# Totals of the adaLN vectors over the partitions: VectorE transposes and row sums with one 32-column matmul, in place of eight one-column matmuls

## The chip, the cores and the metric

One core of one Trainium2 chip runs the whole program. The metric is the device time of one execution in microseconds (us); the kernel before took 1523.76 us, the median of 3 runs between 1518.08 and 1527.92.

## The reference, cut to what matters

The program is one inference step of a two-layer hybrid backbone. It has 128 context tokens and 256 latent tokens of width 2048. Each layer multiplies normalised tokens by a large input projection (2048 x 7184), runs four branches (a linear recurrence, neighbourhood attention, grouped attention, a matrix memory) and goes through an output projection (2048 x 2048). What the change touches is the adaLN modulation:

```python
mod = jax.nn.silu(cond) @ lp['ada_w'] + lp['ada_b']
shift, scale, gate = jnp.split(mod, 3, axis=-1)
xm = rmsnorm(x, lp['norm_w']) * (1.0 + scale) + shift
...
x = x + gate * y
```

There are two conditioning vectors (context and latent), so per layer this is a product of 2 x 2048 with 2048 x 6144, all in float32. The input projection needs scale and shift of a channel before it can read it; the output step needs the gate.

## The kernel before, in words

**Large matmuls.** Both projections run on TensorE in three float32 passes (high x high, low x high, high x low), issued by `block` (line 1321) and, for the last 256 output columns, by `mm` (line 1362). The weights arrive in `raw`; ScalarE writes their high part `wh` (line 190 is the helper `act`), GpSimd their low part `wl` (line 1218). Tokens are modulated channel block by channel block in `modulate`: VectorE writes `xmt` and the low part `xl` (line 194 is the helper `stt`), ScalarE the high part `xh`.

**The adaLN vectors.** The 6144 outputs of a layer are cut into 12 sets of 512 columns: sets 0 to 7 hold shift and scale for 256 channels each, sets 8 to 11 the gate. Set 0 of layer 0 is made on TensorE (`ada_pe`). The other 23 sets are made on VectorE. For each of the 16 blocks of 128 input rows the weights `araw` (128 x 512) are multiplied by the conditioning value of each partition and added to an accumulator in PSUM, `sbp`: `ada_dve` puts two such pieces, one for each conditioning vector c, into a list called `backlog`. The last piece of a set writes to SBUF (`adasb`, 128 x 1024) instead. What is left is the total over the 128 partitions. `ada_final` (line 300) makes it with eight matmuls: each takes 128 columns of `adasb` as the stationary operand and one column of ones as the moving one, so that 128 totals come out as a column in PSUM. Line 305 adds the bias into `mod`, and one more instruction makes `Amul` for the scales.

**What sets the order.** A list called `plan` interleaves the visits of the projection with the adaLN pieces: 2.5 blocks per visit in layer 0, 2.0 in layer 1 (`RATE`), so that the vectors for the next channel group are due three visits ahead (`LAG`). After each block of matmuls `tick` takes an eighth of the backlog, at least one entry, and starts each final whose time has come (`FLAG` later than its last piece). Where a visit needs a channel that is not modulated yet, `need` and `ada_wait` empty the backlog and run the finals at that place. Layer 0 reads its channels in groups of 2, 2, 2, 2, 4 and 4 blocks (`KG`), and needs sets 1 to 7 during its first pass over the weights. Layer 1 has two groups of 8 blocks; its sets 0 to 3 and the gates of layer 0 run beside the later part of layer 0. Each engine then works through its own queue in order. While layer 0 makes its first sums the final's PSUM bank is also one that the projection uses (`final_bank`), so that the next block waits until VectorE has read it.

**Start.** The constants `cst` (identity and ones, 128 x 256) are loaded from ScalarE's queue (line 1463) while SyncE's queue loads conditioning, adaLN weights and tokens.

Of the kernel before, what the change touches and what calls it, by code (L numbers as in the profile page):

```python
# [9 lines left out]
F32 = mybir.dt.float32  # L10
F32R = mybir.dt.float32r
AF = mybir.ActivationFunctionType
OP = mybir.AluOpType
AX = mybir.AxisListType
# [4 lines left out]
T = TP + TS  # L19
DEPTH = 2  # L20
# [10 lines left out]

CC = {}
_n = 0
for _name, _w in (("ident", 128), ("ones", 128), ("u", 128), ("l", 128), ("mf", 128), ("mb", 128),
                  ("cos", 256), ("sin", 256), ("nam", 64)):
    CC[_name] = (_n, _n + _w)
    _n += _w
# [8 lines left out]
PP_W = _n  # L46
# [3 lines left out]
def shape_consts():  # L50
    a = np.zeros((128, CC_W), np.float32)
    p = np.arange(128)

    def put(name, v):
        a[:, CC[name][0]:CC[name][1]] = v

    put("ident", np.eye(128))
    put("ones", 1.0)
    put("u", p[:, None] <= p[None, :])
    put("l", p[:, None] >= p[None, :])  # L60
    put("mf", np.where(p[:, None] > p[None, :], BIG, 0.0))
    put("mb", np.where(p[:, None] < p[None, :], BIG, 0.0))
    qc, kc = p % 64, np.arange(64)
    st = np.clip(qc - 8, 0, 48)[:, None]
    put("nam", np.where((kc[None] >= st) & (kc[None] < st + 16), 0.0, NEG))
    inv = np.float32(10000.0) ** (-np.arange(32, dtype=np.float32) / np.float32(32))
    t = np.arange(256)
    ang = [(q.astype(np.float32)[:, None] * inv).astype(np.float32) for q in (t // 64, t % 64)]
    cos = np.concatenate([np.cos(ang[0]), np.cos(ang[0]), np.cos(ang[1]), np.cos(ang[1])], 1)
    sin = np.concatenate([-np.sin(ang[0]), np.sin(ang[0]), -np.sin(ang[1]), np.sin(ang[1])], 1)  # L70
    put("cos", cos.reshape(2, 128, 128).transpose(1, 0, 2).reshape(128, 256))
    put("sin", sin.reshape(2, 128, 128).transpose(1, 0, 2).reshape(128, 256))
    return a
# [3 lines left out]
def tile_hybrid_step(ctx: ExitStack, tc: tile.TileContext, I, O):  # L77
    nc = tc.nc
    ps_space = bass.MemoryType.PSUM
    consts = ctx.enter_context(tc.tile_pool(name="consts", bufs=1))  # L80
# [3 lines left out]
    wrk = ctx.enter_context(tc.tile_pool(name="wrk", bufs=1))  # L84
# [6 lines left out]
    FLAG = 4.0  # L91
# [12 lines left out]
    clock = dict(now=0.0, due=0.0)  # L104
    deferred = []
    backlog = []
# [36 lines left out]
    def sm(i, n, name):  # L143
        return wrk.tile([128, n], F32, name=name, tag=f"m{i}", bufs=2)

    pers_all = consts.tile([128, T + 256 + PP_W + DEPTH * 128 + 256], F32, name="pers")
    used = [0]

    def pers(n):
        used[0] += n  # L150
        return pers_all[:, used[0] - n:used[0]]

    cst = pers(256)
    prm = pers(PP_W)
    nc.sync.dma_start(prm[:, :PP_1], I["prm"][:, :PP_1])

# [3 lines left out]
    def C(n):  # L160
        return cst[:, CC[n][0]:CC[n][1]]

    def P(n, l=None, parts=2):
        a, b = PP[n]
        if l is None:
            return prm[:, a:b]
        s = (b - a) // parts
        return prm[:, a + l * s:a + (l + 1) * s]

    ident = C("ident")  # L170
    ones = C("ones")
# [16 lines left out]
    def act(out, in_, f, bias=0.0, scale=1.0, accum=None):  # L188
        if accum is None:
            return nc.scalar.activation(out, in_, f, bias=bias, scale=scale)  # L190
        return nc.scalar.activation(out, in_, f, bias=bias, scale=scale, accum_out=accum)  # L191

    def stt(out, a, s, b, op0, op1):
        return nc.vector.scalar_tensor_tensor(out, a, s, b, op0=op0, op1=op1)  # L194
# [41 lines left out]
    ada_acc = dict(done=0)  # L236
    last_ev = {}

    def order(later, earlier):
        tc.add_manual_dep(later, earlier.name,  # L240
                          mybir.DependencyInfo(mybir.DependencyClass.NoSync, mybir.DependencyReason.DATA),
                          reason="issue order")
# [22 lines left out]
    sbp = pada.tile([128, 1024], F32, name="sbp")  # L265

    def ada_pe(it):
# [8 lines left out]
        if it["stop"]:  # L276
# [7 lines left out]
                ada_final_mod(0, j0, 2)  # L284
            ada_acc["done"] += 1

    finals = []
    rot = [True]

    def final_bank():  # L290
        if not rot[0]:
            return scr("adaf")
        turn[0] += 1
        return (accb[3], sbank[1])[turn[0] % 2]

    def ada_final(l, s, part):
        pt = final_bank()
        for q in range(4):
            for c in range(2):
                nc.tensor.matmul(pt[:, 2 * q + c:2 * q + c + 1], part[:, c * 512 + q * 128:c * 512 + q * 128 + 128],  # L300
                                 ones[:, 0:1], start=True, stop=True)
        pv = pt[:, 0:8].rearrange("p (q c) -> p q c", c=2)
        for j0, q0, n in (((2 * s, 0, 2), (16 + 2 * s, 2, 2)) if s < 8 else ((4 * s, 0, 4),)):
            b = P("ada_b", l)[:, j0:j0 + n]
            nc.vector.tensor_tensor(mod[:, l, j0:j0 + n, :], pv[:, q0:q0 + n, :],  # L305
                                    b[:, :, None].to_broadcast([128, n, 2]), op=OP.add)
            if 16 <= j0 < 32:
                nb = P("norm", l)[:, j0 - 16:j0 - 16 + n]
                stt(Amul[:, l, j0 - 16:j0 - 16 + n, :], mod[:, l, j0:j0 + n, :], 1.0,
                    nb[:, :, None].to_broadcast([128, n, 2]), OP.add, OP.mult)  # L310
        ada_acc["done"] += 1
        ada_acc[l, s] = True
# [5 lines left out]
    def ada_dve(it):  # L318
        raw = it["raw"]

        def piece(c):
            it["left"] -= 1
            l, s, k = it["l"], it["s"], it["k"]
            acc = sbp[:, c * 512:(c + 1) * 512]
            sc = scond[:, k, c:c + 1]
            if it["start"]:
                d = nc.vector.tensor_scalar(acc, raw, sc, None, op0=OP.mult)
            elif not it["stop"]:
                d = stt(acc, raw, sc, acc, OP.mult, OP.add)
            else:  # L330
                if c == 0:
                    ada_acc["part"] = wrk.tile([128, 1024], F32, name="adasb", tag="adasb", bufs=1)
                part = ada_acc["part"]
                d = stt(part[:, c * 512:(c + 1) * 512], raw, sc, acc, OP.mult, OP.add)
                if c == 1:
                    finals.append((clock["now"] + FLAG, lambda: ada_final(l, s, part)))
            if "v" in last_ev:
                order(d.ins, last_ev["v"])

        it["left"] = 2  # L340
        for c in range(2):
            backlog.append(lambda c=c: piece(c))

    def ada_wait(ok):
        while not ok():
            if backlog:
                drain_backlog(1)
            elif finals:
                run_finals(True)
            else:  # L350
                run_deferred(True)
# [1109 lines left out]
            pos[key] += 1  # L1461

    nc.scalar.dma_start(cst, I["cst"])
    act(warm, scond[:, 0, 0:1], AF.Sqrt, bias=epsc, scale=0.0)
    pos["a"] = n_first
    xq = [range(k, k + 4) for k in range(0, KC, 4)]
    for tok in START:
        if tok == "x":
            for k in xq[0]:
                nc.sync.dma_start(xr[k], I["xT"][:, k, :])  # L1470
            for k in xq.pop(0):
                square_in(k, xr[k], nc.vector)
        elif tok == "w":
            upto("w", wl, w_dma, pos["w"] + 1)
        elif tok == "r":
            rstd_bc()
        elif tok == "P":
            it = first.pop(0)
            a_dma(it)
            ada_pe(it)  # L1480
        elif tok == "D":
            it = a_items[pos["a"]]
            upto("a", a_items, a_dma, pos["a"] + 1)
            ada_dve(it)
            it["early"] = True
# [4 lines left out]
    for it in plan:  # L1490
# [3 lines left out]
        if ty == "a":  # L1494
            upto("a", a_items, a_dma, it["i"] + NADA - 1)
            (ada_pe if it["mode"] == "pe" else ada_dve)(it)
        elif ty == "mod":
            l = it["l"]
# [19 lines left out]
        else:  # L1518
# [6 lines left out]
            if open_banks and PRE[it["l"]] and not it["first"]:  # L1525
                open_banks = False
                for t in [accb[nb] for nb in PREB] + [sbank[0]]:
                    nc.tensor.matmul(t, xh[0][:, 0:128], xh[0][:, 0:1].to_broadcast([128, 512]),
                                     start=True, stop=True)
# [22 lines left out]
def lay_out(inp):  # L1552
# [36 lines left out]
    put("m0", f["state_mlstm_m"][0].reshape(1, -1))  # L1589
    a["prm"] = p  # L1590
    k = shape_consts()
    a["cst"], a["mlk"], rope, nam = np.split(k, (CC["u"][0], CC["cos"][0], CC["nam"][0]), 1)
    a["gqk"] = np.stack([np.concatenate([rope, np.broadcast_to(f["gqa_qnorm"][l], (128, 128)),
# [49 lines left out]
```

## Time and profile before

| | before |
|---|---|
| median of 3 runs | 1523.76 us |
| profiled execution, its own time | 1518.68 us |
| its span on the core | 1516.9 us |
| TensorE matmul (PE) busy | 1448.2 us, 95% |
| VectorE (DVE) busy | 1003.0 us, 66% |
| GpSimd (POOL) busy | 930.0 us, 61% |
| ScalarE (ACT) busy | 793.5 us, 52% |
| mean granted TensorE clock | 0.976 |

Busy shares are of the span. A profile gives each instruction's start and duration, and for an engine that stood idle the instruction or transfer that ended the wait. Matmuls overlap each other, so the time that one takes of TensorE is read from start to start, not from its duration. A float32 matmul shows as two passes, each with its own weight load.

### The profile page before, as it was taken

To read this page: it belongs to the slowest core of one execution; us is meant where nothing else is said; L and a number is where in the kernel's file an instruction comes from. 1 tells how busy PE (TensorE), PEld (TensorE's weight loads), DVE (VectorE), ACT (ScalarE), POOL (GpSimd) and SP (SyncE) were. 2 spreads that over 40 slices of the span, in tenths; PEclk is the share of its full clock that TensorE was granted. 3 is DMA by queue.
4 is the path that set the end of the run, shared out by engine and by line. 5 is a ranking of instruction groups with operands and counts; after the bars stand their busy time and mean duration, and the time that the engine had idled before them with its cause. 6 is when DMAs were issued, how large, how long until landed. Compare 5 with 4: busy or idle time off the path is not lost. (4 is left out here: it accounts for less than half of the span.)

```text
span 1516.9 us, 24338 instructions
## 1 busy us (share of the span) xinstructions
PE 1448.2 (95%) x8321; PEld 1364.1 (90%) x8321; DVE 1003.0 (66%) x1858; ACT 793.5 (52%) x1613; POOL 930.0 (61%) x1270
## 2 busy tenths in 40 slices
PE   6999989999997899999999999999999989899997
PEld 1989979999986798999998999999999869899997
DVE  4988988887759777655558995644844864643423
ACT  4689945664456773632334343233444876364432
POOL 1656655656657658556647665775656775845762
PEclk7999989999999999999999999999999999999999
DMA  8877867866646474476747886654545445435543
GB/s 278 269 246 231 253 203 234 258 189 196 173 124 181 122 224 135 150 231 218 251 140 255 254 254 181 188 165 120 155 138 154 130 134 164 138 103 184 180 126 95
DMA packets 167165, 281.64 MB, mean 186 GB/s; under 512 B 17216, under 2 KB 48960, under 8 KB 166912
## 3 DMA queue, kind: packets, MB, share of 16 engines
q1 hardware_dynamic: 159520, 272.40, 58.6%
q10 hardware_dynamic: 7296, 7.42, 1.5%
q8 instruction: 65, 1.06, 0.3%
q14 instruction: 60, 0.49, 0.1%
q0 software_dynamic: 224, 0.27, 0.1%
HBM read 271.11 MB, written 8.93 MB: 185 GB/s over the span
## 5 line engine op out<-in xcount | busy, mean ns | idle before, releaser
L1218 POOL TENSOR_TENSOR wl<-raw,wh 128x256 fp32r<-128x256 f32 (+1 forms) x1152 | 857.9, 777 | 496.7 <-ACT wh L190 450.8
L1321 PE MATMUL acc<-xh,wh 128*128 128x384 f32 x1634 | 564.4, 346 | 13.2 <-ACT xh L190 6.7
L1321 PE MATMUL acc<-xl,wh 128*128 128x384 f32 x1634 | 556.4, 340 | 1.2 <-DVE xl L194 1.2
L1321 PE MATMUL acc<-xh,wl 128*128 128x384 f32 x1634 | 553.2, 339 | 2.4 <-POOL wl L1218 2.4
L190 ACT ACTIVATE wh<-raw 128x1024 fp32r<-128x1024 f32 (+2 forms) x304 | 307.1, 1014 | 408.4 <-PE acc L1321 331.0
L194 DVE SCALAR_TENSOR_TENSOR sbp<-araw,pers,sbp 128x512 f32<-128x512 f32 x644 | 484.0, 752 | 21.9 <-DMA araw<-in_ada_n 8.8
L1321 PEld LDWEIGHTS acc<-xh,wh 128*128 128x128 f32 x1634 | 308.9, 189 | 18.5 <-ACT xh L190 7.9
L1321 PEld LDWEIGHTS acc<-xh,wl 128*128 128x128 f32 x1634 | 308.6, 189 | 3.8 <-POOL wl L1218 3.5
L1321 PEld LDWEIGHTS acc<-xl,wh 128*128 128x128 f32 x1634 | 309.2, 189 | 2.8 <-DVE xl L194 1.5
L1321 PE MATMUL acc<-wh,xl 128*128 128x512 f32 (+2 forms) x454 | 165.2, 364 | 3.4 <-DVE xl L194 3.1
L1321 PE MATMUL acc<-wh,xh 128*128 128x512 f32 (+2 forms) x454 | 164.1, 362 | 0.0
L1321 PE MATMUL acc<-wl,xh 128*128 128x512 f32 (+2 forms) x454 | 162.9, 359 | 0.0
L1321 PEld LDWEIGHTS acc<-wh,xl 128*128 128x128 f32 x454 | 87.3, 192 | 17.7 <-DVE xl L194 4.8
L1321 PEld LDWEIGHTS acc<-wl,xh 128*128 128x128 f32 x454 | 87.7, 193 | 11.3
L1321 PEld LDWEIGHTS acc<-wh,xh 128*128 128x128 f32 x454 | 87.7, 193 | 10.6
L194 DVE SCALAR_TENSOR_TENSOR cat<-acc,pers,xold 128x128 f32<-128x128 f32 (+1 forms) x56 | 20.6, 409 | 111.9 <-PE acc L1321 111.8
L190 ACT ACTIVATE xh<-xmt,pers 128x128 fp32r<-128x128 f32 x72 | 29.0, 430 | 41.0 <-DVE xmt L194 40.9
L190 ACT ACTIVATE cat<-acc 128x384 f32<-128x384 f32 (+1 forms) x78 | 38.3, 496 | 6.8 <-PE acc L1321 6.0
L300 PEld LDWEIGHTS s<-pers,adasb 128*128 128x128 f32 x304 | 37.3, 193 | 2.3 <-ACT arena L191 1.7
L305 DVE TENSOR_TENSOR pers<-s,pers 128x4 f32<-128x4 f32 (+1 forms) x30 | 4.0, 158 | 50.7 <-PE s L300 47.7
L300 PE MATMUL s<-pers,adasb 128*128 128x1 f32 x304 | 35.7, 246 | 1.4 <-DVE adasb L194 1.3
L194 DVE SCALAR_TENSOR_TENSOR xl<-xmt,pers,xh 128x128 fp32r<-128x128 f32 x72 | 35.3, 511 | 1.7 <-ACT xh L190 1.6
(334 smaller groups left out, 1823.3 us busy)
## 6 DMA issues: line engine op xcount, KB each, us to landing
raw<-in_w_in SPq DMA_DIRECT2D x208, 512.0 KB, 3.9
araw<-in_ada_n SPq DMA_DIRECT2D x368, 256.0 KB, 4.3
raw<-in_w_out SPq DMA_DIRECT2D x64, 512.0 KB, 3.7
raw<-in_w_in SPq DMA_DIRECT2D x32, 256.0 KB, 3.0
araw<-in_ada_n SPq DMA_DIRECT2D x8, 512.0 KB, 5.6
xr<-in_xT SPq DMA_DIRECT2D x16, 192.0 KB, 5.1
nac<-in_nac SPq DMA_DIRECT2D x8, 288.0 KB, 4.1
xold<-in_xT SPq DMA_DIRECT2D x3, 768.0 KB, 6.3
```

The source lines that it names most:

```text
L190: return nc.scalar.activation(out, in_, f, bias=bias, scale=scale)
L194: return nc.vector.scalar_tensor_tensor(out, a, s, b, op0=op0, op1=op1)
L300: nc.tensor.matmul(pt[:, 2 * q + c:2 * q + c + 1], part[:, c * 512 + q * 128:c * 512 + q * 128 + 128], ones[:, 0:1], start=True, stop=True)
L305: nc.vector.tensor_tensor(mod[:, l, j0:j0 + n, :], pv[:, q0:q0 + n, :], b[:, :, None].to_broadcast([128, n, 2]), op=OP.add)
L1218: nc.gpsimd.tensor_tensor(it["lo"][:, kk, cs], raw[:, kk, cs], hv[:, kk, cs], op=OP.subtract)
L1321: last_ev["pe"] = nc.tensor.matmul(out, a, b, start=s0 and i == 0, stop=s1 and i == 2, skip_group_check=not it["first"]).ins
```

## The change

The stationary operand and the moving one change places, and VectorE shortens the moving one first.

1. The last piece of a set now stays in the accumulator `sbp` in PSUM; `adasb` as a 128 x 1024 tile is gone.
2. A new entry of the backlog, `fold`, runs once for each conditioning vector. It transposes the 128 x 512 accumulator in blocks of 32 x 32 from PSUM to SBUF (`turned`), and sums each block's rows, so that 16 columns are left per vector: `red` is 128 x 32.
3. `ada_final` makes one matmul: a constant 128 x 128 matrix `sel` (one where two partitions have the same number modulo 32) times `red`, 32 columns. Its output still holds four candidates per total; VectorE multiplies by the mask `quarter` and sums groups of four (`picked`). The bias addition follows as before.
4. `cst` grows from 128 x 256 to 128 x 384 by `sel`. `quarter` is made once at the start by a VectorE reduction of the identity, ahead of the first sums of squares.
5. The final is entered into its list by the second fold, not by the last piece.

```diff
--- before.py
+++ after.py
@@ -31,7 +31,7 @@
 
 CC = {}
 _n = 0
-for _name, _w in (("ident", 128), ("ones", 128), ("u", 128), ("l", 128), ("mf", 128), ("mb", 128),
+for _name, _w in (("ident", 128), ("ones", 128), ("sel", 128), ("u", 128), ("l", 128), ("mf", 128), ("mb", 128),
                   ("cos", 256), ("sin", 256), ("nam", 64)):
     CC[_name] = (_n, _n + _w)
     _n += _w
@@ -56,6 +56,7 @@
 
     put("ident", np.eye(128))
     put("ones", 1.0)
+    put("sel", p[:, None] % 32 == p[None, :] % 32)
     put("u", p[:, None] <= p[None, :])
     put("l", p[:, None] >= p[None, :])
     put("mf", np.where(p[:, None] > p[None, :], BIG, 0.0))
@@ -143,14 +144,14 @@
     def sm(i, n, name):
         return wrk.tile([128, n], F32, name=name, tag=f"m{i}", bufs=2)
 
-    pers_all = consts.tile([128, T + 256 + PP_W + DEPTH * 128 + 256], F32, name="pers")
+    pers_all = consts.tile([128, T + 384 + PP_W + DEPTH * 128 + 264], F32, name="pers")
     used = [0]
 
     def pers(n):
         used[0] += n
         return pers_all[:, used[0] - n:used[0]]
 
-    cst = pers(256)
+    cst = pers(384)
     prm = pers(PP_W)
     nc.sync.dma_start(prm[:, :PP_1], I["prm"][:, :PP_1])
 
@@ -284,6 +285,7 @@
                 ada_final_mod(0, j0, 2)
             ada_acc["done"] += 1
 
+    quarter = pers(4)
     finals = []
     rot = [True]
 
@@ -293,13 +295,16 @@
         turn[0] += 1
         return (accb[3], sbank[1])[turn[0] % 2]
 
-    def ada_final(l, s, part):
+    def ada_final(l, s, red):
         pt = final_bank()
-        for q in range(4):
-            for c in range(2):
-                nc.tensor.matmul(pt[:, 2 * q + c:2 * q + c + 1], part[:, c * 512 + q * 128:c * 512 + q * 128 + 128],
-                                 ones[:, 0:1], start=True, stop=True)
-        pv = pt[:, 0:8].rearrange("p (q c) -> p q c", c=2)
+        nc.tensor.matmul(pt[:, 0:32], C("sel"), red, start=True, stop=True)
+        picked = sm(14, 40, "picked")
+        pv = picked[:, 32:40].rearrange("p (c q) -> p q c", c=2)
+        nc.vector.tensor_tensor(picked[:, 0:32].rearrange("p (g a) -> p g a", a=4),
+                                pt[:, 0:32].rearrange("p (g a) -> p g a", a=4),
+                                quarter[:, None, :].to_broadcast([128, 8, 4]), op=OP.mult)
+        nc.vector.tensor_reduce(picked[:, 32:40], picked[:, 0:32].rearrange("p (g a) -> p g a", a=4),
+                                axis=AX.X, op=OP.add)
         for j0, q0, n in (((2 * s, 0, 2), (16 + 2 * s, 2, 2)) if s < 8 else ((4 * s, 0, 4),)):
             b = P("ada_b", l)[:, j0:j0 + n]
             nc.vector.tensor_tensor(mod[:, l, j0:j0 + n, :], pv[:, q0:q0 + n, :],
@@ -325,21 +330,31 @@
             sc = scond[:, k, c:c + 1]
             if it["start"]:
                 d = nc.vector.tensor_scalar(acc, raw, sc, None, op0=OP.mult)
-            elif not it["stop"]:
+            else:
                 d = stt(acc, raw, sc, acc, OP.mult, OP.add)
-            else:
-                if c == 0:
-                    ada_acc["part"] = wrk.tile([128, 1024], F32, name="adasb", tag="adasb", bufs=1)
-                part = ada_acc["part"]
-                d = stt(part[:, c * 512:(c + 1) * 512], raw, sc, acc, OP.mult, OP.add)
-                if c == 1:
-                    finals.append((clock["now"] + FLAG, lambda: ada_final(l, s, part)))
             if "v" in last_ev:
                 order(d.ins, last_ev["v"])
+
+        def fold(c):
+            l, s = it["l"], it["s"]
+            acc = sbp[:, c * 512:(c + 1) * 512]
+            if c == 0:
+                ada_acc["red"] = sm(15, 32, "red")
+            red = ada_acc["red"]
+            turned = wrk.tile([128, 512], F32, name="turned", tag="adasb", bufs=2)
+            d = nc.vector.transpose(turned, acc)
+            nc.vector.tensor_reduce(red[:, c * 16:(c + 1) * 16], turned.rearrange("p (g i) -> p g i", i=32),
+                                    axis=AX.X, op=OP.add)
+            if "v" in last_ev:
+                order(d.ins, last_ev["v"])
+            if c == 1:
+                finals.append((clock["now"] + FLAG, lambda: ada_final(l, s, red)))
 
         it["left"] = 2
         for c in range(2):
             backlog.append(lambda c=c: piece(c))
+        for c in range(2 if it["stop"] else 0):
+            backlog.append(lambda c=c: fold(c))
 
     def ada_wait(ok):
         while not ok():
@@ -1461,6 +1476,7 @@
             pos[key] += 1
 
     nc.scalar.dma_start(cst, I["cst"])
+    nc.vector.tensor_reduce(quarter, ident.rearrange("p (a i) -> p a i", i=32), axis=AX.X, op=OP.add)
     act(warm, scond[:, 0, 0:1], AF.Sqrt, bias=epsc, scale=0.0)
     pos["a"] = n_first
     xq = [range(k, k + 4) for k in range(0, KC, 4)]
```

## Rows read from the trace of the kernel before

**Rows 1.** Engine busy by stretch: us, PE, PEld, DVE, ACT, POOL (instructions), PEclk, DMA, GB/s.
```profile
57.00:274.00 217.00, 208.90 (x1205) 199.59 (x1204) 194.59 (x318) 158.74 (x366) 122.76 (x172) 0.96 0.76 233
274.00:400.00 126.00, 126.00 (x774) 123.01 (x773) 97.43 (x197) 72.07 (x161) 83.33 (x115) 1.00 0.70 212
400.00:600.00 200.00, 182.35 (x966) 161.79 (x965) 145.65 (x271) 120.04 (x258) 131.12 (x172) 0.97 0.52 156
```

**Rows 2.** Groups by form on PE, line 300: count | busy us, mean ns | idle before.
```profile
L300 PE MATMUL s<-pers,adasb 128*128 128x1 f32 x304 | 35.7, 246 | 1.4 <-DVE adasb L194 1.3
L300 PE MATMUL acc<-pers,adasb 128*128 128x1 f32 x64 | 9.4, 270 | 1.0 <-DVE adasb L194 0.9
```

**Rows 3.** Timeline of PE and DVE around one set: start us, us, instruction, count.
```profile
348.59 1.41 DVE L194 SCALAR_TENSOR_TENSOR adasb<-araw,pers,sbp 128x512 f32<-128x512 f32 x2
...
355.02 1.84 PE L300 MATMUL s<-pers,adasb 128*128 128x1 f32 x16
356.72 0.42 PE L1321 MATMUL acc<-xh,wh 128*128 128x384 f32 x1
```

**Rows 4.** Timeline of PE: two-pass matmuls of 129 columns in a row.
```profile
426.11 0.38 PE L745 MATMUL s<-ml_v,arena 128*128 128x129 f32 x2
426.33 0.39 PE L746 MATMUL s<-ml_v,arena 128*128 128x129 f32 x2
```

**Rows 5.** Groups by form on DVE: count | busy us, mean ns | idle before.
```profile
L194 DVE SCALAR_TENSOR_TENSOR adasb<-araw,pers,sbp 128x512 f32<-128x512 f32 x46 | 32.4, 741 | 0.6 <-DMA araw<-in_ada_n 0.2
...
L840 DVE TENSOR_TENSOR_SCAN arena<-arena,pers 128x256 f32<-128x256 f32 x16 | 16.8, 1047 | 0.0
...
L1015 DVE TENSOR_REDUCE nm<-s 128x1 f32<-128x384 f32 x16 | 8.3, 549 | 1.3 <-PE s L1012 1.3
...
L305 DVE TENSOR_TENSOR pers<-s,pers 128x4 f32<-128x4 f32 x22 | 2.7, 156 | 28.8 <-PE s L300 28.8
...
L1015 DVE TENSOR_REDUCE nm<-s 128x1 f32<-128x128 f32 x8 | 2.3, 282 | 15.7 <-PE s L1010 15.7
...
L502 DVE TENSOR_TENSOR ml_v<-acc,ml_v 128x512 f32<-128x512 f32 x3 | 2.1, 691 | 8.2 <-PE acc L1321 8.2
```

**Rows 6.** Waits of DVE between 57 and 274 us: total us, times, longest.
```profile
DVE pers L305 <- PE acc L300: 7.4, 4, 2.5
DVE cat L1290 <- PE acc L1321: 4.4, 3, 3.5
DVE pers L305 <- PE s L300: 3.2, 2, 2.0
```

**Rows 7.** Timeline around a set of the first pass; PE and DVE.
```profile
227.75 1.41 DVE L194 SCALAR_TENSOR_TENSOR adasb<-araw,pers,sbp 128x512 f32<-128x512 f32 x2
...
230.26 1.62 PE L300 MATMUL acc<-pers,adasb 128*128 128x1 f32 x14
...
231.92 0.16 DVE L305 TENSOR_TENSOR pers<-acc,pers 128x4 f32<-128x4 f32 x1 [1.97 <-PE acc L300]
```

**Rows 8.** Tile adasb, all 23 sets: idle of PE and PEld before line 300, us, times.
```profile
  DVE adasb L194: 4.2, 5
```

**Rows 9.** Timeline: a tight set beside the neighbourhood attention, PE.
```profile
526.89 0.35 PE L300 MATMUL s<-pers,adasb 128*128 128x1 f32 x2 [1.33 <-DVE adasb L194]
```

**Rows 10.** Timeline: last modulation of set 7, and the visit that reads it.
```profile
268.94 0.74 DVE L194 SCALAR_TENSOR_TENSOR xl<-xmt,pers,xh 128x128 fp32r<-128x128 f32 x2
...
274.03 0.29 PE L1321 MATMUL acc<-wh,xl 128*128 128x272 f32 x1
```

**Rows 11.** Timeline of PE at a set of layer 1.
```profile
1040.97 2.19 PE L300 MATMUL s<-pers,adasb 128*128 128x1 f32 x16
```

**Rows 12.** Line 1321 by stretch: us, PE (instructions), PEld (instructions), PEclk, DMA, GB/s.
```profile
1035.00:1042.00 7.00, 5.04 (x28) 4.42 (x26) 1.00 0.56 161
1042.00:1049.00 7.00, 5.05 (x15) 4.68 (x16) 0.52 0.27 89
```

**Rows 13.** Timeline of DVE at the start.
```profile
13.01 5.20 DVE L372 TENSOR_TENSOR arena<-arena,sq 128x384 f32<-128x384 f32 x8 [9.08 <-ACT sq L190]
```

## The prediction

> **What bounds the kernel now.** I read the shares of the engines first, then the same by stretch, then the timeline around a set, because a mean over stages hides who is last in each. TensorE is busy for nearly the whole span. By stretch [rows 1] it is busy all 126 of 126 us from 274 to 400, 208.9 of 217 in the first pass over the weights, and 182 of 200 where attention runs, so there it waits for a chain of other engines. VectorE is busy 194.6 of 217 us in the first pass: there both engines are nearly full, and an addition to VectorE can cost what a removal from TensorE brings. Elsewhere VectorE has room.
>
> **The matmuls that go.** The 23 sets show 304 and 64 passes [rows 2], 16 per set, two for each of the eight matmuls. The duration of 246 ns is no price, since passes overlap. From start to start the 16 take 356.72 - 355.02 = 1.70 us [rows 3], 106 ns per pass. The new matmul has two passes of 32 columns; no row shows that size, but two passes of 129 columns follow each other within 426.33 - 426.11 = 0.22 us [rows 4], as long as two passes of one column, so I take 0.22 (bounds 0 and, if 32 columns cost as much again as 129, 0.44). A set saves 1.70 - 0.22 = 1.48 us of TensorE, 23 sets 34.0 us.
>
> A rule against this saving stands in the Trainium skill, TensorE: Matmul & The Clock Gate, Back-to-back issue gap: a matmul of 1 to 64 columns needs about 60 cycles, some 25 ns, from the last one. By it the 16 passes would take 0.4 us, and all 23 sets could save at most 9 us (an estimate from that page), and the sum below would stand at -11.5 + 25 = +13.5 us. The trace has 1.70 us, which leaves that no chance; the same page, under LDWEIGHTS, ties the weight load to its 128 columns (107 ns), and the measured 106 ns is that one. I go by the rows.
>
> **What VectorE gets.** Per set: two transposes of 128x512 out of PSUM, two row sums of 128x512, one product and one sum of 32 columns. The trace has no transpose on this engine. The nearest row is an operation that reads 512 columns of PSUM, 0.691 us [rows 5]; from below it could not be less than the 0.282 of 128 columns, as no row streams faster; from above I take twice the scan of 256 columns, 2 x 1.047 = 2.1 us, the slowest row per column. I take 0.69: the rows of a plain pass lie together, the scan is a recurrence. Row sums: 549 ns at 384 columns and 282 at 128 are 1.04 ns per column, so 0.68 at 512. The product of 32 columns: 0.156 at 4 columns plus 28 x 1.04 ns, 0.19; the sum of 32: 0.282 less 96 x 1.04 ns, 0.18. Together 1.38 + 1.36 + 0.37 = 3.11 us per set, 72 us in all. The last piece costs as before (0.741), it only writes elsewhere.
>
> The Trainium skill has a price for the transpose. VectorE: DVE Perf Modes, The three transpose paths, gives 311 ns for 128x128 in a 16-bit type; with one element per cycle (Vector Engine (DVE) Microarchitecture Reference, 3.8) that is an estimate of 0.71 us for 512 columns, and the sum would move by less than 1 us. No row here shows it.
>
> **First pass, 57 to 274 us, seven sets.** VectorE's work becomes 194.6 + 7 x 3.11 = 216.4 us. It idled 22.4 us; 7.4 + 3.2 = 10.6 of that was waiting for the eight matmuls [rows 6], which I put at 0.6 per set from now on, 4.2 us; of the remaining 11.8 us I keep 5, as waits for projection blocks (4.4) shrink when VectorE runs late. That is 225.6 us, 8.6 more than the stretch. What it must meet is the visit at 274.03, and the last modulation for it ends at 268.94 + 0.74 = 269.68 [rows 10]: 4.35 us are free. So **+4** us. Bounds: if all idle time stays, 216.4 + 22.4 - 217 - 4.35 = +17; if VectorE keeps up, TensorE gains 7 x 1.48 = -10. In these sets the final stands directly behind the last piece [rows 7]: now two transposes and two row sums come between them, and behind the final's wait on VectorE stand the next set's pieces and the modulation that TensorE reads.
>
> **Sixteen later sets.** In twelve the matmuls come after VectorE is done, as at 355.02 with the pieces done at 350.0 [rows 3], and the removed time is TensorE's own: 12 x 1.48 = **-17.8** us. Four are tight: at 526.89 TensorE waited for the piece [rows 9] (five such waits in all, 4.2 us [rows 8]). From last piece to totals took 1.70 us and will take 2.74 + 0.22 = 2.96, so each lies between +1.26, if TensorE stands still, and -1.48, if other blocks go ahead; I take +0.5, **+2** in all. In the attention stretches VectorE is a link of the chain that TensorE waits for; four sets there put 3.1 us each into its queue. Bounds 0 and 3.1 each, I take 0.5: **+2**.
>
> **Clock.** At 1040.97 the 16 one-column passes run 2.19 us [rows 11]; in the next 7 us the granted clock is 0.52, so TensorE runs at 1.2 of its 2.4 GHz, and line 1321 gets 15 passes done against 28 before [rows 12]. 7 x 0.48 = 3.4 us are lost. Nothing else idles TensorE there, so without the long run of one-column work I expect the fall to be gone, but not surely: **-2** (bounds 0 and -3.4).
>
> **Start.** The reduction for the mask (0.28 us) waits for the constants at the head of VectorE's queue, which stands idle for 9.08 us then [rows 13]; without that cover it would cost its 0.28. The constants are 64 KB longer, 0.28 us at 233 GB/s [rows 1] beside the first product's weights: **+0.3**.
>
> **Sum.** 4 - 17.8 + 2 + 2 - 2 + 0.3 = -11.5 us against the profiled execution's 1518.68, so 1507.2. The median of the runs, 1523.76, is 5.1 us above it; taken over to it, 1512.
>
> **The rivals.** (a) *The whole gain arrives.* VectorE's waits for finals (10.6 us in the first pass) vanish and absorb the folds: 23 x -1.48 - 3.4 + 0.3 = -37, 1487. For it: VectorE idles half of what it gets; against it: the seven sets in the first pass are tight. From -19 to -38.
> (b) *VectorE takes it all back.* If the first pass stands at its upper bound (+17 in place of +4) the sum is +1.5, 1525. For it: 90% busy there; against it: the 4.35 us free.
> (c) *Slower: the transpose is slow.* Each further us of a transpose costs 14 us in the first pass, 8 in the tight sets and 4 in the attention sets, 26 in all. From 0.69 + 11.5 / 26 = 1.13 us on the kernel is slower; at 2.1 us the sum is -11.5 + 26 x 1.41 = +25, 1549. For it: no row of a transpose; against it: every row of a plain pass.
> (d) *The change doesn't do what it says.* If the folds sit so late in the backlog that TensorE stands still for all seven first-pass and four tight sets, it is 11 x 1.26 - 17.8 + 2 - 2 + 0.3 = -4, which (b) and the forecast cover.
>
> **How the numbers follow.** Forecast (-4 to -19) 0.47; (a) 0.26; (b) with (d), -4 to +8, 0.14; (c) 0.13. From 1523.76, 1% is 15.2 us, about what a measurement can tell from none. Faster: (a) 0.26 and the part of the forecast below -15.2, about a quarter, 0.13, so 0.39. Slower: three quarters of (c), where the transpose is above 1.72 us, 0.10. Within 1%: 0.51. The range leaves out the last us of (a) and (c) above 1%: -35 to +15, 1489 to 1539. The forecast alone is 1505 to 1520.
>
> **What would show it.** Two passes per set in place of 16, 46 in all, and 0.22 us for them; 46 transposes near 0.69 us, row sums near 0.68; VectorE near 216 us in the first pass with the visit now at 274 about 4 us later; no fall of the clock behind the set at 1041; TensorE's waits for the fold only in the first pass and four sets. A transpose over 1.1 us, or the first-pass visit earlier than 274, would make the prediction wrong in its steps; TensorE waiting in the twelve loose sets would make it wrong in its largest term.

## The result, and the profile after

The changed kernel takes 1503.22 us (median of 4 runs, 1501.84 to 1505.05) against 1524.89 us of the kernel before (4 runs, 1518.08 to 1527.92). The ratio is 0.986, with a 95% interval of 0.984 to 0.988: 1.4% faster, 21.7 us between the medians. The profiled executions lie nearer together, 1518.68 and 1504.49 us, spans 1516.9 and 1502.7: the execution profiled before lies 6 us below its kernel's median of these runs. What follows compares those two traces, which are 14.2 us apart; where the rest of the 21.7 us lies, no trace shows.

The busy times on the first page of the profile after: engine, busy us and share of the span, instructions.

```profile
span 1502.7 us, 23812 instructions
PE 1411.3 (94%) x7999; PEld 1324.0 (88%) x7999; DVE 1066.6 (71%) x1997; ACT 793.9 (53%) x1613; POOL 929.5 (62%) x1270
```

TensorE has 322 matmul passes less, which is 23 sets of 14. VectorE is busy 63.6 us longer, against 1003.0 before, which is 2.77 us for each of the 23 sets. What it does now, groups by form on DVE with count, busy us and mean ns:

```profile
L345 DVE STREAM_TRANSPOSE turned<-sbp 128x512 f32<-128x512 f32 x46 | 30.6, 696 | 0.7
L346 DVE TENSOR_REDUCE red<-turned 128x16 f32<-128x512 f32 x46 | 28.8, 660 | 0.1
...
L306 DVE TENSOR_REDUCE picked<-picked 128x8 f32<-128x32 f32 x23 | 4.1, 180 | 0.2
L303 DVE TENSOR_TENSOR picked<-s,pers 128x32 f32<-128x32 f32 x20 | 3.7, 187 | 16.6 <-PE s L300 16.4
```

The transpose takes 0.696 us, the row sum 0.660, product and sum of 32 columns 0.19 and 0.18. On TensorE the new matmul stands in the timeline of the profile after (start us, us):

```profile
538.05 0.30 PE L300 MATMUL s<-red,pers 128*128 128x32 f32 x2
538.19 0.48 PE L1336 MATMUL acc<-wh,xh 128*128 128x512 f32 x1
```

From its start to the next matmul it is 0.14 us, where the sixteen passes took 1.70 [rows 3]; a set gives back 1.56 us of TensorE. It is 0.14 us in 17 of the 23 sets; in five sets in front of which TensorE had waited it is 0.24, and 1.01 at set 5, at the lower clock and with a wait of 0.4 in it.

Time by stage is read at three visits of 272 columns: the last channel group of layer 0, the start of layer 1 and its second group. In the timeline after, first pass of each:

```profile
280.33 0.29 PE L1336 MATMUL acc<-wh,xl 128*128 128x272 f32 x1
...
789.93 0.29 PE L1336 MATMUL acc<-wh,xl 128*128 128x272 f32 x1
...
933.02 0.29 PE L1336 MATMUL acc<-wh,xl 128*128 128x272 f32 x1
```

and in the timeline before, where the first of the three is the one at 274.03 [rows 10]:

```profile
789.59 0.29 PE L1321 MATMUL acc<-wh,xl 128*128 128x272 f32 x1
...
938.76 0.29 PE L1321 MATMUL acc<-wh,xl 128*128 128x272 f32 x1
```

So the first pass, with seven sets, ends 6.3 us late. The rest of layer 0 (eight sets) takes 509.6 us in place of 515.6, the first group of layer 1 (four sets) 143.1 in place of 149.2, and what follows (four sets) 569.7 in place of 578.1. Sum, from the unrounded times: +6.3 - 6.0 - 6.1 - 8.5 = -14.2 us.

Where the first pass loses is one place, the matmul of set 5. Timeline after, PE and DVE:

```profile
206.35 1.31 DVE L345 STREAM_TRANSPOSE turned<-sbp 128x512 f32<-128x512 f32 x2
207.59 1.24 DVE L346 TENSOR_REDUCE red<-turned 128x16 f32<-128x512 f32 x2
...
208.88 0.64 PE L300 MATMUL s<-red,pers 128*128 128x32 f32 x2 [13.33 <-DVE red L346]
```

TensorE stands still for 13.3 us until VectorE has the row sums. In the kernel before, set 5 began here:

```profile
197.82 3.81 PE L300 MATMUL acc<-pers,adasb 128*128 128x1 f32 x16 [0.93 <-DVE adasb L194]
```

So set 5 comes 11.1 us late. From there to the end of the pass it is 71.4 us in place of 76.2, so that 4.8 us are won back behind it and 6.3 are left. VectorE itself hardly waits in the first pass any more: from 57 to 274 us it is busy 203.75 us where it was 194.59 [rows 1], and its waits for the final are

```profile
DVE picked L303 <- PE acc L300: 1.6, 3, 0.7
...
DVE picked L303 <- PE s L300: 0.5, 2, 0.3
```

2.1 us in place of 10.6 [rows 6]. Behind the set at 1038 the granted clock no longer falls. Engine busy by stretch after (us, PE, PEld, DVE, ACT, POOL, PEclk, DMA, GB/s):

```profile
1038.00:1045.00 7.00, 7.00 (x48) 6.70 (x47) 6.89 (x21) 4.82 (x13) 3.07 (x5) 1.00 0.36 117
```

against 0.52 behind the same set before [rows 12]. Around set 5, though, the granted clock is 0.75 from 200 to 240 us, where it was 0.88. Before and after:

```profile
200.00:240.00 40.00, 37.94 (x208) 36.79 (x209) 35.09 (x61) 21.75 (x42) 20.38 (x29) 0.88 0.71 221
```

```profile
200.00:240.00 40.00, 28.04 (x140) 26.83 (x141) 38.06 (x64) 16.48 (x33) 14.95 (x22) 0.75 0.66 206
```

The mean clock over the span is 0.974, no better than 0.976.

### The profile page after: what moved, and what is told of

Its sections match the earlier page's. It is cut to its first block, busy times and chain, and to the rows that moved or that the text cites. A ratio compares the mean times of both kernels' runs of the same rounds, so it can differ in the third digit from the quotient of the medians.

```text
span 1502.7 us, 23812 instructions
## 1 busy us (share of the span) xinstructions
PE 1411.3 (94%) x7999; PEld 1324.0 (88%) x7999; DVE 1066.6 (71%) x1997; ACT 793.9 (53%) x1613; POOL 929.5 (62%) x1270
## 5 line engine op out<-in xcount | busy, mean ns | idle before, releaser
L195 DVE SCALAR_TENSOR_TENSOR sbp<-araw,pers,sbp 128x512 f32<-128x512 f32 x690 | 518.5, 751 | 19.6 <-DMA araw<-in_ada_n 6.3
L1336 PE MATMUL s<-xh,wh 128*128 128x384 f32 x92 | 32.3, 351 | 5.1 <-ACT xh L191 4.4
L387 DVE TENSOR_TENSOR arena<-arena,sq 128x384 f32<-128x384 f32 x38 | 25.2, 664 | 16.0 <-ACT sq L191 14.7
L332 DVE TENSOR_SCALAR sbp<-araw,pers 128x512 f32<-128x512 f32 x46 | 34.4, 747 | 0.4
```

Of the source, the lines that this page charges most:

```text
L387: eng.tensor_tensor(sqacc, sqacc, s, op=OP.add)
L1336: last_ev["pe"] = nc.tensor.matmul(out, a, b, start=s0 and i == 0, stop=s1 and i == 2, skip_group_check=not it["first"]).ins
```

## The experiments

Theory A: the removed passes are TensorE's own time wherever VectorE has room, and in the first pass VectorE is the bound, so that its added work comes back as time there. The rivals are named in the expectations. The table has, for each kernel, the start of set 5's matmuls, the end of the first pass (the visit at 274.03 before), the time from there to the end, the span, and the ratio of times to before with its interval. The times are of one profiled execution each, in us; the ratio is of the medians, each kernel beside its own runs of the kernel before.

| kernel | set 5 starts | first pass ends | rest | span | ratio |
|---|---|---|---|---|---|
| before | 197.8 | 274.0 | 1242.9 | 1516.9 | 1 |
| the change | 208.9 | 280.3 | 1222.4 | 1502.7 | 0.986 (0.984 to 0.988) |
| e1: eight matmuls in the first pass | 200.9 | 277.6 | 1216.1 | 1493.7 | 0.982 (0.981 to 0.984) |
| e2: eight matmuls in later sets | 209.2 | 280.3 | 1245.2 | 1525.5 | 1.001 (0.999 to 1.002) |
| e3: fold left out | 199.6 | 271.6 | 1217.6 | 1489.1 | 0.978 (0.976 to 0.979) |
| e4: the eight matmuls twice | 217.8 | 304.2 | 1290.4 | 1594.6 | 1.050 (1.048 to 1.051) |
| e5: merged fold | 208.6 | 280.3 | 1219.5 | 1499.8 | 0.985 (0.982 to 0.988) |
| e6: e1 with merged fold | 198.2 | 274.6 | 1215.0 | 1489.6 | 0.979 (0.976 to 0.982) |
| e7: transposes twice | 218.7 | 290.4 | 1226.5 | 1516.9 | 0.997 (0.996 to 0.999) |
| e8: the change again | 208.4 | 279.4 | 1221.5 | 1500.9 | 0.987 (0.984 to 0.989) |
| e9: eight matmuls in set 5 | 205.4 | 278.9 | 1220.3 | 1499.2 | 0.985 (0.981 to 0.988) |

**The two halves: e1 and e2.** Both kernels hold both ways and choose by set.

```diff
+    def by_ones(l, s):
+        return l == 0 and s < 8          # e2: not (l == 0 and s < 8)
...
+        if by_ones(l, s):
+            for q in range(4):
+                for c in range(2):
+                    nc.tensor.matmul(pt[:, 2 * q + c:2 * q + c + 1], red[c][:, q * 128:q * 128 + 128], ones[:, 0:1], ...)
...
+            elif it["stop"] and by_ones(l, s):
+                part = wrk.tile([128, 512], F32, name="adasb", tag="adasb", bufs=2)
+                it.setdefault("part", []).append(part)
+                d = stt(part, raw, sc, acc, OP.mult, OP.add)
...
+        for c in range(2 if it["stop"] and not by_ones(it["l"], it["s"]) else 0):
```

> Sets 1 to 7 of layer 0 make their totals with the eight one-column matmuls as before, the 16 later sets as in the change. Theory A (the first pass is VectorE's, the later sets are TensorE's own time): the visit that the change moved from 274.1 to 280.4 us is back at 274, the 16 later sets keep the 20 us that they won, so the span is 1502.7 - 6.3 = 1496 us and the ratio to before about 0.982. Rival B (the stall of the first pass is made up later anyway, so only the lost 7 x 1.48 us count): span about 1513 us, ratio 0.993.

> The other half: transposes and row sums in sets 1 to 7 of layer 0 only, the eight matmuls in the 16 later sets. Theory A: the first pass ends 6 us late and nothing is won behind it: span 1516.9 + 6 = 1523 us, ratio 1.004. Rival B: the first pass wins 7 x 1.48 = 10 us: span 1507 us, ratio 0.993.

e1 came out as theory A had it: a span of 1493.7 us where 1496 was expected, and a ratio of 0.982. e2's span is 1525.5 where 1523 was expected, but that execution lies 4.5 us above the median of its kernel, and the ratio of 1.001 (0.999 to 1.002) shows neither the loss of theory A (1.004) nor the gain of rival B (0.993). Rival B is out in both. The visit that ends the first pass, in the timelines of e1 and then e2:

```profile
277.56 0.29 PE L1352 MATMUL acc<-wh,xl 128*128 128x272 f32 x1
```

```profile
280.32 0.29 PE L1352 MATMUL acc<-wh,xl 128*128 128x272 f32 x1
```

e2 has the change's 280.3 and wins nothing behind it. e1 gets only part of the 6 us back in this execution: its second channel group began 2 us later than in the kernel before (83.7 in place of 81.6 us), and from 82 to 87 us the granted clock was 0.50 where it was 0.88. e6, which has the same first pass, ends it at 274.6. The change pays in the sixteen later sets and only there. By spans the two halves add up to the whole, -23.2 and +8.6 us against -14.2. By medians they don't, -27.3 and -0.2 against -21.7: the profiled execution of before lies below its kernel's median and that of e2 above. So the 6 us that the first pass costs are seen in the traces, and no ratio here shows them for that half alone.

**VectorE's work: e3 and e7.** e3 makes no totals: one copy of 16 columns per vector stands in for transpose and row sum. e7 makes each transpose twice.

```diff
-            d = nc.vector.transpose(turned, acc)
-            nc.vector.tensor_reduce(red[:, c * 16:(c + 1) * 16], turned.rearrange("p (g i) -> p g i", i=32), ...)
+            d = nc.vector.tensor_copy(red[:, c * 16:(c + 1) * 16], acc[:, 0:16])     # e3
...
+            nc.vector.transpose(turned, acc)                                         # e7, ahead of the other
```

> The change with transposes and row sums left out: one copy of 16 columns per vector stands in for them, so the totals are not made. Theory A (VectorE's added work is what holds the first pass back): the first pass wins about 7 x 1.48 = 10 us against before instead of losing 6, and the tight sets win too: span about 1516.9 - 37 = 1480 us, ratio 0.976. Rival C (VectorE's added work lies in its idle time and costs nothing): as the change, 1502 us, ratio 0.986.

> The change with each transpose done twice: 1.4 us more of VectorE per set. The price in the prediction was 26 us of time per us of transpose, 14 of it in the first pass: 0.70 x 26 = 18 us, ratio to before 0.998. Theory A with the measured places of the change (only set 5 stalls TensorE in the first pass, and tight later sets stall it by under 1 us): 5 sets x 1.4 in front of that stall and two or three tight sets, 8 to 11 us, ratio 0.992. Rival C (VectorE's added work lies in idle time): 0.986.

The end of the first pass and TensorE's wait at set 5 in e3, then in e7:

```profile
199.56 0.63 PE L300 MATMUL s<-red,pers 128*128 128x32 f32 x2 [7.16 <-DVE red L344]
...
271.55 0.29 PE L1333 MATMUL acc<-wh,xl 128*128 128x272 f32 x1
```

```profile
218.74 0.63 PE L300 MATMUL s<-red,pers 128*128 128x32 f32 x2 [16.41 <-DVE red L347]
...
290.39 0.28 PE L1337 MATMUL acc<-wh,xl 128*128 128x272 f32 x1
```

VectorE's added work sets when TensorE can go on at set 5. e7 reaches set 5 9.9 us later than the change (218.74 against 208.88). Ten more transposes of 0.70 us lie ahead of it, 7.0 us, so they count there by more than their own length: in e7 VectorE is busy 149.4 us from 57 us to set 5, 141.6 in the change, and idles 12.3 in place of 10.3. Behind set 5 it is different. From there to the end of the pass it is 71.7 us in e7, 71.4 in the change and 72.0 in e3, so four transposes more or all folds less change nothing there. With the eight matmuls it is 76.2 (before), 76.7 (e1) and 76.4 (e6). So VectorE binds the first pass up to set 5, and behind it the time goes with TensorE's passes.

The whole kernel loses 15.2 us to the change beside it (1518.79 against 1503.56), 22 us per us of transpose. That is nearer to the prediction's price of 26 than to the 8 to 11 us that I had revised it to after the change's trace. The revision had the right place, the five sets up to the stall, but 7 us where it is 10, and it had too little for the later sets, which lose 4 to 5 us (rest 1226.5 against 1222.4 and 1221.5).

e3 ends the first pass 8.8 us earlier than the change, and its ratio is 0.978 where the change has 0.986: rival C is out. It is only 2.5 us earlier there than the kernel before, not 10. TensorE reaches set 5 sooner without the long passes and still waits 7.2 us for the plain additions, so that set 5 starts 1.7 us later than before: even without any fold, VectorE is late there.

**TensorE's price: e4.** Each of the eight matmuls of the kernel before is issued twice.

```diff
-        for q in range(4):
+        for q in range(8):
+            q = q % 4
```

> The kernel before with each of the eight one-column matmuls issued twice (the second overwrites the first with the same totals): 16 passes more per set. Theory A (106 ns per pass of TensorE's own time in nearly all sets): 23 x 1.70 = 39 us more, span 1556 us, ratio 1.026, and more falls of the granted clock behind such sets. Rival D (what the change won is not these passes but something beside them): under 15 us more, ratio below 1.01.

It is 74 us slower by medians, twice what I expected. A set's 32 passes take the time that the price says. Two sets in the timeline of e4 (start us, us):

```profile
183.04 4.03 PE L301 MATMUL acc<-pers,adasb 128*128 128x1 f32 x30
...
388.65 3.63 PE L301 MATMUL s<-pers,adasb 128*128 128x1 f32 x32
392.14 0.42 PE L1322 MATMUL acc<-xh,wh 128*128 128x384 f32 x1
```

At 388 it is 3.49 us for 32 passes, 109 ns each, so 23 x 16 more are 40 us. The rest is the clock. This is the granted clock around the set at 183 (us, PE, PEld, DVE, ACT, POOL, PEclk, DMA, GB/s):

```profile
180.00:186.00 6.00, 6.00 (x46) 6.00 (x44) 2.78 (x5) 3.30 (x6) 2.55 (x4) 0.97 0.84 293
186.00:193.00 7.00, 7.00 (x26) 7.00 (x26) 3.00 (x8) 3.07 (x6) 0.22 (x1) 0.54 0.30 81
```

TensorE has no idle time in either stretch, and still the granted clock goes from 0.97 to 0.54, mostly its lower level (1.2 of 2.4 GHz), behind the one-column passes. Over the span, from the view of spans and clock:

```profile
core 0: 1594.6 us, clock 0.951
```

(1 - 0.951) x 1594.6 = 78 us of full clock are lost, against (1 - 0.976) x 1516.9 = 36 before: 42 us more. 40 + 42 = 82, near the 78 us between the spans. Rival D is out: the passes are TensorE's own time.

**The stall in front of set 5: e8 and e9.** e8 is the change itself. e9 is the change with `by_ones` true for set 5 of layer 0 alone.

> The change itself beside the other three on the same chip, as their yardstick: ratio 0.986 and span near 1502 us, and TensorE's long stall again in front of set 5 (13 us). Rival G (that stall belongs to one execution): the stall is gone or elsewhere.

> The change, but set 5 of layer 0, in front of which TensorE stalled 13.3 us, makes its totals with the eight matmuls. Theory A (VectorE is the bound of the whole first pass, and set 5 is only the place where TensorE meets it): VectorE reaches the end of set 5 by 3 us earlier, TensorE's stall there shrinks to about 10 us, the first pass ends at 277 us in place of 280, ratio 0.984. Rival H (the place alone: the fold of set 5 is what TensorE waits for): the stall is gone but for 1 us as in the kernel before, the first pass ends near 270 us, ratio 0.979.

The matmul of set 5 in e8, then the sixteen passes in its place in e9 and the end of the first pass:

```profile
208.35 0.64 PE L300 MATMUL s<-red,pers 128*128 128x32 f32 x2 [13.33 <-DVE red L346]
```

```profile
205.43 3.81 PE L306 MATMUL acc<-pers,adasb 128*128 128x1 f32 x16 [6.20 <-DVE adasb L195]
...
278.90 0.29 PE L1352 MATMUL acc<-wh,xl 128*128 128x272 f32 x1
```

The stall of 13.3 us is there in both profiled executions of the change. With the eight matmuls at that place alone VectorE is ready 2.9 us earlier (205.43 against 208.35), as theory A has it, and the stall halves to 6.2 us. It is not gone, as rival H has it, but the pass ends at 278.9, nearly as late as with the change (280.3 and 279.4), where theory A had 277. TensorE doesn't wait elsewhere for it: behind set 5 its waits are 2.1 us in all, 3.3 in e8. What was won goes into the sixteen passes. The granted clock is 0.50 around them,

```profile
205.00:210.00 5.00, 3.73 (x16) 3.56 (x16) 2.51 (x5) 0.00 (x0) 0.00 (x0) 0.50 0.41 130
```

so they take 3.81 us, and from the start of set 5 to the end of the pass it is 73.5 us in place of 71.1.

**Shorter folds: e5 and e6.** One transpose and one row sum of 1024 columns per set.

```diff
+            if c == 0:
+                return
+            turned = wrk.tile([128, 1024], F32, name="turned", tag="turned", bufs=1)
+            d = nc.vector.transpose(turned, sbp)
+            nc.vector.tensor_reduce(red, turned.rearrange("p (g i) -> p g i", i=32), axis=AX.X, op=OP.add)
```

> The change with one transpose of 128x1024 and one row sum of 1024 columns per set in place of two of each. By the rows (0.70 and 0.67 us at 512 columns, 1.04 ns per column) the pair takes 1.23 + 1.20 us in place of 2.74, 0.3 us less per set. Theory A (VectorE binds the first pass): about 2 us off the first pass, its stall in front of set 5 shorter by as much, ratio to before 0.984. Rival E (the whole set has to be ready before the first half is turned, and tight sets lose what is saved): 0.986 as the change.

> Eight matmuls in sets 1 to 7 of layer 0 and, in the 16 later sets, the matmul of 32 columns behind one merged transpose and one merged row sum. Theory A: the later sets are TensorE's time and VectorE has room there, so the shorter fold adds at most 1 us: ratio 0.982, as with the eight matmuls in the first pass alone. Rival F (the fold still holds the tight later sets): up to 5 us better, 0.979.

The pair in e5, groups by form on DVE:

```profile
L347 DVE STREAM_TRANSPOSE turned<-sbp 128x1024 f32<-128x1024 f32 x23 | 28.7, 1248 | 0.7
L348 DVE TENSOR_REDUCE red<-turned 128x32 f32<-128x1024 f32 x23 | 28.0, 1218 | 0.8
```

By these durations it is 2.47 us in place of 2.71. VectorE's busy time is no shorter, though, 1069.2 us against 1066.6 of the change, and the stall at set 5 isn't either (14.1 us). e5 has 1501.29 us by median against 1503.56 of the change beside it: inside the intervals, theory A and rival E can't be told apart. e6 is the fastest kernel here, 1491.15 us by median, 2.2% under the kernel before. It differs from e5 only in sets 1 to 7 and is 10.1 us faster on the same chip, so that is what the choice by stage brings. Whether the merged fold gave it anything over e1 (0.979 against 0.982) stays open: the intervals overlap, and the two were timed on different chips.

## Why the prediction was right, and where its sizes were off

The prediction was right in sign and range, and its two mechanisms are there: passes that are TensorE's own time in the later sets, and a first pass that VectorE's folds hold back. Forecast was 1512 us, measured 1503.22, within 1489 to 1539. It put 0.51 on "within 1%" and 0.39 on what came, faster by over 1%, and the 20.5 us below 1523.76 lie outside the forecast's own 4 to 19, just inside the band of rival (a). Step by step:

- **Passes that go.** 1.48 us a set was predicted, 1.56 measured; the new matmul takes 0.14 us, less than the 0.22 of 129 columns that I took. e4 shows that the price holds: 109 ns per pass.
- **VectorE's price.** 3.11 us a set was predicted; the durations add up to 2 x 0.696 + 2 x 0.660 + 0.19 + 0.18 = 3.08. The value from the row of a plain pass was right, the scan's far off. Neighbouring instructions overlap a little, so that VectorE's busy time grows by 2.77 us a set, 63.6 in all and not 72. The estimate of 0.71 us that I had from the Trainium skill, VectorE: DVE Perf Modes, The three transpose paths, agrees with the measured 0.696.
- **First pass.** +4 predicted, +6.3 measured (+5.4 in e8). That the size is so near is partly luck, since the path is another. I had VectorE's work of all seven sets run late, with 4.35 us free at the end. VectorE's delay was met at set 5, in one wait of 13.3 us that I had not foreseen: +11.1 us. Behind set 5 TensorE's shorter passes gave back 4.8, a gain that I had only in a bound. VectorE was busy 209.6 us up to the visit, not 216.4, and its waits for finals went from 10.6 to 2.1 us, where I kept 4.2.
- **Later sets.** -17.8 + 2 + 2 - 2 = -15.8 us predicted, -20.5 measured. In the two traces it comes to this: 16 x 1.56 = 25.0 us of passes go, TensorE is idle 50.4 us behind the first pass where it was 45.7, and the lower clock takes 17.3 us where it took 17.5 (one minus the granted clock, times the length, summed over stretches of about 100 us): -25.0 + 4.7 - 0.2 = -20.5. The term that was mis-sized most is that of the tight sets, booked at +0.5 us each: TensorE waits there 0.40 us at 834, 0.51 at 866, 0.22 at 1462, and not at all at 538, so they win as well. What the attention chain cost is some part of the 4.7 us of idle time and can't be told apart; another 1.6 us of it is a wait in a set that I had called loose, at 311. The fall of the clock behind 1041 is gone, 3.4 us where I took 2, but other falls came in its place, so that this term brought next to nothing.
- **Clock over all.** The mean granted clock is not higher (0.974 against 0.976): the first pass has more of the lower clock, around set 5. In e6, which has no such stall, it is 0.982.
- **Carrying the sum to the median.** The sum was 1507.2 us for the profiled execution, which came to 1504.49, a miss of 2.7, in which +2.3 in the first pass and -4.7 behind it partly cancel. Added to the median of before, 5.1 us above its profiled run, it became 1512. The changed kernel's profiled execution lies 1.3 us above its own median instead, so that step makes 6.1 of the 8.8 us of the miss.

Rival (a), the whole gain, came half true: e6, 33 us under the kernel before, shows what it takes, the folds kept out of the stage in which VectorE is full. Rivals (b) and (c) would have needed a first pass 17 us late or a transpose of over 1.13 us. For (c) e7 gives the test: with 1.4 us of transposes per vector the kernel is still at 0.997. At its 22 us per us of transpose, an estimate, the kernel would be slower from about 1.6 us on, not from 1.13.

**The open difference.** Behind the first pass e1 is 6.3 us faster than the change with the same later sets (1216.1 against 1222.4). Part is the lag that VectorE carries on: in the change TensorE waits at the first later set too,

```profile
311.00 0.41 PE L300 MATMUL s<-red,pers 128*128 128x32 f32 x2 [1.60 <-DVE red L346]
```

and in e1 it does not. Most of it goes with the clock: by the same sum over stretches the lower clock takes 17.3 us behind the first pass in the change, 11.8 in e1 and 11.7 in e6. The stretch with the largest difference, in the change and then in e1:

```profile
500.00:600.00 100.00, 94.35 (x477) 84.10 (x476) 72.21 (x144) 60.93 (x135) 67.27 (x92) 0.95 0.50 150
```

```profile
500.00:600.00 100.00, 91.71 (x492) 83.16 (x491) 82.39 (x150) 59.05 (x133) 72.88 (x97) 0.98 0.54 163
```

Why the clock falls less often there, with the same later sets, is not shown.

## What to carry to other kernels

An exchange between two engines has to be priced by stage: in the profiled executions the same edit paid 20 us where VectorE had room and cost 6 where it had none, and choosing by stage brought nearly half as much again as doing it everywhere (33.0 us in e6, 22.8 in e5 beside it). A long wait of one engine at one place can be where the lag of another shows, and not what causes it. In e9 the wait halved, but the sixteen passes that replaced the fold took that time themselves, and the end of the pass moved by about a microsecond. A stage can also change its bound on the way: here VectorE set the time up to set 5 and TensorE behind it. Cutting the stage at the wait, in the timelines of several kernels, is what showed it. And one profiled execution can lie several microseconds off its kernel's median, so a sum made against it should be compared as a difference.

## What the runs showed of the hardware

- In a run, one-column float32 passes took as much of TensorE as passes of 129 columns: 106 to 109 ns per pass at the full clock, against 110. A single pair took 0.14 us with 32 columns, and a single pair of one column the same (229.16 to 229.30 us in the kernel before).
- Doubling the runs of one-column passes from 1.7 to 3.5 us cost about twice their own length: 40 us of passes and 42 us of a lower granted clock, with no idle time of TensorE in the stretch shown (180 to 193 us).
- VectorE's 32x32 transpose of 128x512 float32 from PSUM took 0.696 us and of 128x1024 1.248 us, by these two an estimate of 1.08 ns per column beside a fixed 0.14 us.
